# Token-major recurrence inputs, merge blocks between the recurrence's parts, modulation pieces moved, and a fixed order of the up products

## The chip, the cores and the metric

The kernel runs on one core of one Trainium2 chip. The metric is the device time of one execution in microseconds (us). The kernel before was timed three times: 1805.51 us is the median, 1804.99 to 1805.75 the range. A further execution was recorded by the profiler; all rows below come from it.

## The reference, cut to what matters

One block of a hybrid network on 256 tokens of width 2048, all in float32:

```python
mod = silu(c) @ ada_w + ada_b            # six vectors: sh1, sc1, g1, sh2, sc2, g2
h = rmsnorm(x, norm1_g) * (1 + sc1) + sh1
q, kc, vc, ks, vs, kw, vw, gates, lx, ly, ga, gb = split(h @ w_in)
o_a = nsa_attention(q, kc, vc, ks, vs, kw, vw, gates, ...)   # 16 heads, 4 groups
u = causal_dwconv(lx, conv_w, conv_b)
o_b = gelu(ly) * rg_lru(u, w_a, b_a, w_i, b_i, lam)          # a scan over the tokens
merged = sigmoid(ga) * (o_a @ proj_a) + sigmoid(gb) * (o_b @ proj_b)
x = x + g1 * (merged @ w_out)
h = rmsnorm(x, norm2_g) * (1 + sc2) + sh2
gate, val = split(h @ w_up)
x = x + g2 * ((gelu(causal_dwconv(gate)) * val) @ w_down)
return rmsnorm(x, final_g)
```

`lx` and `ly` are 2048 wide each. The recurrence wants them with the features on the partitions and the tokens along the row, since its scan runs along the row. `proj_a` needs the attention alone, `proj_b` the recurrence alone, the gates `ga` and `gb` only `h`.

## The kernel before

**How a weight is used.** Every weight comes from HBM in pieces of 128x2048 floats (1 MB) into a ring of four buffers `raw`. `stage` (line 95) issues the load on SP's queue; all loads keep their program order there. `split` (line 100) makes of each half piece (128x1024) a rounded part `hi` (ScalarE, line 107) and a rest `lo` (VectorE, line 108); three buffers of each exist. A product in the chip's float32r form is then three terms: `hi` of one side with `hi` and `lo` of the other, and `lo` with `hi`. The activations `h1`, `oA`, `oB`, `mg`, `h2` lie in SBUF with their rounded part in columns 0 to 255 (one per token) and the rest in columns 256 to 511.

**Two forms of a product.** Feature-major: the weight is the stationary side (128x128), the tokens move, and the result has features on the partitions. `dense_pair` (line 114) does so with one matmul of 512 columns (`hi` against both halves of the tokens, line 130) and one of 256 (`lo`, line 131). `dense_pair1` (line 171) makes 256 output features in one PSUM bank, by three matmuls of 256 columns for each weight tile (lines 184, 186, 187): 24 for each half piece. Token-major: `dense_tok` (line 191) has the tokens stationary and 512 columns of the weight moving; it makes 512 output features for 256 tokens in two banks by 12 matmuls of 512 columns for each half piece (lines 202 to 204), so 96 for the four pieces of one block. The dense products share four PSUM banks (tag "d", line 112), given out in turn; a bank comes free when the engine that empties it has read it.

**Stages.** Keys, values, queries and the first gate columns (`mq`) come first, then attention in eight units (`attention(g, t)`, four head groups by two token halves) beside the last quarter of those products and the products for `lx` (loop at line 682: eight pairs, each with two pieces, the bank copied by ScalarE in line 684). The recurrence follows in four parts `bt` of 512 features (line 694): a convolution on VectorE, two small float32 products for its gates (lines 713, 715), sigmoid, tanh, exp and sqrt on ScalarE (their order fixed by `tbl`, as each change of function loads a table), scans on VectorE, then twice a `dense_pair1` for `ly`, its gelu (line 735), the product with the scan, and the split into `oB`. Then the merge (line 749): for each of four output blocks `n` of 512 features and for each side `s`, the gate (for `n` = 0 already in `mq`, otherwise a `dense_tok`), its sigmoid (line 760), the projection by `dense_tok`, their product (line 763); the two sides are added and turned by float32 transposes on PE (line 774) into `mg`. `w_out`, the up products (`up`, line 151; 42 of the 48 by `dense_pair`) and the down products follow.

**Modulation pieces.** The first two of the six vectors are needed at once; the other 64 pieces (`filler`, `ada_piece`, line 230) take a `raw` buffer and 1 MB of load each and are multiplied and summed by VectorE alone (line 233). Before, 16 stand in the `lx` loop, 4 in the recurrence, 28 in the merge (in twos and fours behind a projection), 16 in the up stage.

**Order.** Each engine runs its instructions in one fixed order. A list scheduler with a timing model sets it when the kernel is built, from program order and priorities (`high_priority`); only what `keep_in_program_order` names keeps the order of the text.

## Time and profile before

| | us |
|---|---|
| median of 3 runs | 1805.51 (1804.99 to 1805.75) |
| the profiled execution's own time | 1807.09 |
| its span, first to last instruction | 1804.9 |
| PE busy | 1784.9 (99%) |
| weight loads busy | 1556.1 (86%) |
| VectorE (DVE) busy | 1340.6 (74%) |
| ScalarE (ACT) busy | 870.4 (48%) |
| HBM traffic | 429.51 MB moved, mean 238 GB/s |

PE is TensorE's matmuls, PEld its weight loads, which overlap them. Matmuls are pipelined: the duration of one is longer than the distance from its start to the next start, so a busy share of 99% doesn't say how many products were streamed in that time; the distance of starts does.

### The profile page before, as it was taken

Reading aid. Unit: us, or ns where it says so; the run is one execution under the profiler, and the core shown is the slowest. Engines: PE = TensorE matmul, PEld = TensorE weight load, DVE = VectorE, ACT = ScalarE, POOL = GpSimd, SP = SyncE. Lnnn points to the kernel's source line nnn. Section 1 sums busy time; section 2 is a strip of 40 time slices with the busy share of each in tenths; the row PEclk is TensorE's granted clock in tenths of the full one; section 3 lists DMA queues with packets and bytes.
Section 4 is the critical chain, followed back from the end, with each engine's and each line's share of the span. In section 5 each row is a group of like instructions: output and inputs, shape, how many; then the busy total and the mean of one; then the engine's idle time right before and its main releaser. Section 6 shows DMA issues by size and latency. Waiting matters only on the chain.

```text
span 1804.9 us, 25840 instructions
## 1 busy us (share of the span) xinstructions
PE 1784.9 (99%) x10336; PEld 1556.1 (86%) x10336; DVE 1340.6 (74%) x1955; ACT 870.4 (48%) x1185; POOL 0.2 (0%) x4
## 2 busy tenths in 40 slices
PE   8999999999999999999999999999999999999998
PEld 7899898888999888888888998888888888888886
DVE  7999876988788766766765997888545666666555
ACT  5644534655578443444445644444433444444443
POOL 0000000000000000000000000000000000000000
PEclk9999999999999999999999999999999999999999
DMA  9999863666546867787775566777655555555553
GB/s 352 362 329 366 312 239 118 210 222 219 215 170 227 289 241 288 289 287 280 292 276 198 184 227 238 274 280 279 244 187 196 189 190 191 188 189 188 186 191 113
DMA packets 64201, 429.51 MB, mean 238 GB/s; under 512 B 7089, under 2 KB 7377, under 8 KB 15569
## 3 DMA queue, kind: packets, MB, share of 16 engines
q1 hardware_dynamic: 63792, 427.08, 66.4%
q8 instruction: 81, 1.33, 0.3%
q10 hardware_dynamic: 288, 0.79, 0.1%
q14 instruction: 40, 0.32, 0.0%
HBM read 425.72 MB, written 2.11 MB: 237 GB/s over the span
## 4 chain that ended last, share of the span: by engine, by line
PE 92%; DVE 3%; DMA 2%; ACT 2%; issue 1%; DVEq 0%; ACTq 0%
PE P L130 17%; PE P L203 12%; PE P L204 11%; PE P L202 11%; PE P L131 9%; PE P L186 3%; PE P L187 3%; PE P L184 3%; PE P L437 2%; PE P L439 2%; PE P L438 2%; PE P L431 1%; PE P L432 1%; PE P L430 1%; DMA raw<-ada_w 1%; PE P L148 1%
## 5 line engine op out<-in xcount | busy, mean ns | idle before, releaser
L108 DVE TENSOR_TENSOR lo<-raw,hi 128x1024 fp32r<-128x1024 f32 x589 | 717.9, 1221 | 385.8 <-ACT hi L107 384.4
L107 ACT ACTIVATE hi<-raw 128x1024 fp32r<-128x1024 f32 x589 | 622.8, 1060 | 789.6 <-PE P L204 313.0
L130 PE MATMUL P<-h,hi 128*128 128x512 f32 x1344 | 465.9, 397 | 0.0
L131 PE MATMUL P<-h,lo 128*128 128x256 f32 x1344 | 362.8, 280 | 0.0
L130 PEld LDWEIGHTS P<-h,hi 128*128 128x128 f32 x1344 | 246.8, 188 | 53.2
L131 PEld LDWEIGHTS P<-h,lo 128*128 128x128 f32 x1344 | 253.6, 189 | 7.7
L233 DVE SCALAR_TENSOR_TENSOR raw<-raw,crow 128x2048 f32<-128x2048 f32 x64 | 146.3, 2286 | 7.2 <-DMA raw<-ada_w 6.4
L187 PE MATMUL P<-h,lo 128*128 128x256 f32 x512 | 147.6, 289 | 0.8 <-DVE lo L108 0.8
L186 PE MATMUL P<-h,hi 128*128 128x256 f32 x512 | 146.7, 287 | 0.0
L184 PE MATMUL P<-h,hi 128*128 128x256 f32 x512 | 146.7, 287 | 0.0
L437 PE MATMUL P<-h,hi 128*128 128x256 f32 x384 | 108.3, 286 | 0.0
L438 PE MATMUL P<-h,hi 128*128 128x256 f32 x384 | 107.5, 284 | 0.0
L439 PE MATMUL P<-h,lo 128*128 128x256 f32 x384 | 102.0, 283 | 0.0
L187 PEld LDWEIGHTS P<-h,lo 128*128 128x128 f32 x512 | 97.8, 191 | 1.8 <-DVE lo L108 1.4
L186 PEld LDWEIGHTS P<-h,hi 128*128 128x128 f32 x512 | 97.9, 191 | 1.4 <-issue 1.2
L184 PEld LDWEIGHTS P<-h,hi 128*128 128x128 f32 x512 | 97.9, 191 | 1.0 <-issue 0.7
L203 PE MATMUL P<-lo,ua 128*128 128x512 f32 x240 | 93.4, 389 | 0.0
L204 PE MATMUL P<-hi,ua 128*128 128x512 f32 x240 | 93.4, 389 | 0.0
L202 PE MATMUL P<-hi,ua 128*128 128x512 f32 x240 | 83.6, 389 | 0.0
L203 PE MATMUL P<-lo,h 128*128 128x512 f32 x192 | 75.5, 393 | 0.6 <-DVE lo L108 0.6
L204 PE MATMUL P<-hi,h 128*128 128x512 f32 x192 | 74.9, 390 | 0.0
L437 PEld LDWEIGHTS P<-h,hi 128*128 128x128 f32 x384 | 74.1, 193 | 0.2
(272 smaller groups left out, 3122.5 us busy)
## 6 DMA issues: line engine op xcount, KB each, us to landing
raw<-ada_w SPq DMA_DIRECT2D x96, 1024.0 KB, 5.1
raw<-w_up SPq DMA_DIRECT2D x96, 1024.0 KB, 4.9
raw<-w_down SPq DMA_DIRECT2D x48, 1024.0 KB, 4.9
raw<-w_lru SPq DMA_DIRECT2D x32, 1024.0 KB, 5.0
raw<-w_proj SPq DMA_DIRECT2D x32, 1024.0 KB, 5.0
raw<-w_gates SPq DMA_DIRECT2D x24, 1024.0 KB, 7.3
raw<-w_out SPq DMA_DIRECT2D x16, 1024.0 KB, 5.0
raw<-w_kv SPq DMA_DIRECT2D x24, 512.0 KB, 6.9
```

Source lines behind the costliest of these rows:

```text
L107: A.activation(hi[:, :n], raw[:, lo_col:lo_col + n], AF.Copy)
L108: V.tensor_tensor(lo[:, :n], raw[:, lo_col:lo_col + n], hi[:, :n].bitcast(F32), op=ALU.subtract)
L130: PE.matmul(ps[f], hi[:, sl], r, start=(kt == 0), stop=False, skip_group_check=True)
L131: PE.matmul(o, lo[:, sl], r[:, 0:256], start=False, stop=(kt == n - 1), skip_group_check=True)
L184: PE.matmul(o, hi[:, sl], r[:, 0:256], start=(kt == 0 and f == 0), stop=False, skip_group_check=True)
L186: PE.matmul(o, hi[:, sl], r[:, 256:512], start=False, stop=False, skip_group_check=True)
L187: PE.matmul(o, lo[:, sl], r[:, 0:256], start=False, stop=(kt == n - 1), skip_group_check=True)
L202: PE.matmul(ps[j], xh, hi[:, w], start=(kt == 0), stop=False, skip_group_check=True)
L203: PE.matmul(ps[j], xh, lo[:, w], start=False, stop=False, skip_group_check=True)
L204: PE.matmul(ps[j], xl, hi[:, w], start=False, stop=(kt == n - 1), skip_group_check=True)
L233: V.scalar_tensor_tensor(raw, raw, 1.0, row, op0=ALU.mult, op1=ALU.mult, accum_out=modc[:, c:c + 1])
L437: PE.matmul(o, hi[:, sl], h1[:, kt, 0:256], start=first and f % 2 == 0, stop=False, skip_group_check=True)
```

## The change

- `lx` and `ly` are made by `dense_tok`, in four blocks of 512 features each; the weights are laid out for it on the host. Each block's two banks are copied to SBUF by ScalarE (for `ly` by the gelu) and turned by the new `turned`, eight float32 transposes into two more banks of the same four. For `lx` ScalarE copies the turned banks out; for `ly` VectorE multiplies them with the scan straight from PSUM. `dense_pair1` is gone.
- Merge blocks stand between the parts of the recurrence: behind part 0 the projection of the attention for `n` = 0, behind part 1 the gate (1, 0), whose sigmoids run among those of part 2, behind part 2 the projection of the attention for `n` = 1. The sigmoids of `mq` run among those of part 0.
- Modulation pieces: 7 stand with the last key, value and gate products, 9 with `lx`, 32 in merge blocks, each behind a single piece of a `dense_tok` (two or three in a block); 16 remain for the up stage as before.
- In `dense_pair` the order of the matmuls is written out and kept: with two `hi` products at first in the first half piece, in plain alternation in all others.

The `w_lru` loads stay 32 pieces of 1 MB.

```diff
-        def dense_pair(pieces, rhs, narrow=False):
+        def dense_pair(pieces, rhs):
...
-                    hi, lo = split(raw, half * 1024, 1024)
...
+                    hl = split(raw, half * 1024, 1024)
+                    done = [0, 0]
+                    for w in (0, 0, 1, 0, 1, 0, 1, 1) + (0, 1) * 4 if ip + half == 0 else (0, 1) * 8:
+                        f, k = done[w] // 4, done[w] % 4
+                        done[w] += 1
+                        kt = ip * 8 + half * 4 + k
+                        r = rhs(kt)
+                        tc.keep_in_program_order(
+                            PE.matmul(ps[f][:, 0:256] if w else ps[f], hl[w][:, k * 256 + f * 128:k * 256 + f * 128 + 128],
+                                      r[:, 0:256] if w else r, start=(kt == 0 and not w), stop=(kt == n - 1 and w == 1),
+                                      skip_group_check=True))
...
-        def dense_pair1(pieces, rhs):
...
-        def dense_tok(pieces, lhs, late=None):
+        def dense_tok(pieces, lhs, late=None, fills=()):
...
+                if ip in fills:
+                    filler()
...
+        def turned(rows):
+            ps = [bank("turn"), bank("turn")]
+            for f in range(4):
+                for j in range(2):
+                    o = (f % 2) * 256 + j * 128
+                    PE.transpose(ps[f // 2][:, o:o + 128], rows[:, j, f * 128:f * 128 + 128], ident)
+            return [p.rearrange("p (f t) -> p f t", f=2) for p in ps]
...
         for i in range(4):
             whole(i, 3)
+            filler()
...
             whole(8 + b, 3)
+            filler()
...
-        for pr in range(8):
-            pl = dense_pair1([w_lru[pr, k] for k in range(2)], h1r)
-            A.activation(lx[pr // 2][:, 2 * (pr % 2):2 * (pr % 2) + 2],
-                         pl.rearrange("p (f t) -> p f t", f=2), AF.Copy)
-            if units:
-                attention(*units.pop(0))
-            filler(2)
...
+        for bt in range(4):
+            ps = dense_tok([w_lru[bt, k] for k in range(4)], h1r, fills=(1, 3))
+            rows = lx[bt].rearrange("p (j a) t -> p j (a t)", j=2)
+            for j in range(2):
+                A.activation(rows[:, j], ps[j], AF.Copy)
+            for h, p in enumerate(turned(rows)):
+                A.activation(lx[bt][:, 2 * h:2 * h + 2], p, AF.Copy)
+            for _ in range(2):
+                if units:
+                    attention(*units.pop(0))
+        assert not units
+        filler()
...
+        FILLS = (1, 3)
...
+        def open_gates(n, s, ps):
+            for j in range(2):
+                tbl(A.activation(gated[n, s][j], ps[j], AF.Sigmoid))
+
+        def multiply(n, s):
+            rhs = (lambda kt: oB[kt // 2][:, kt % 2]) if s else (lambda kt: oA[:, kt])
+            ps = dense_tok([w_proj[n, s, k] for k in range(4)], rhs, fills=(0, 1, 3) if s else FILLS)
+            for j in range(2):
+                V.tensor_tensor(gated[n, s][j], ps[j], gated[n, s][j], op=ALU.mult)
+
+        waiting = [(0, s, gates_of(0, s)) for s in range(2)]
...
+            while waiting:
+                open_gates(*waiting.pop(0))
             tbl(A.activation(r, r, AF.Exp, scale=-2.0))
...
-            for h in range(2):
+            ps = dense_tok([w_lru[4 + bt, k] for k in range(4)], h1r)
+            rows = u.rearrange("p (j a) t -> p j (a t)", j=2)
+            for j in range(2):
+                tbl(A.activation(rows[:, j], ps[j], AF.Gelu_apprx_tanh))
+            for h, p in enumerate(turned(rows)):
                 pr = bt * 2 + h
-                pl = dense_pair1([w_lru[8 + pr, k] for k in range(2)], h1r)
                 gl = u[:, 2 * h:2 * h + 2]
-                tbl(A.activation(gl, pl.rearrange("p (f t) -> p f t", f=2), AF.Gelu_apprx_tanh))
-                V.tensor_tensor(gl, gl, iu[:, 2 * h:2 * h + 2], op=ALU.mult)
+                V.tensor_tensor(gl, p, iu[:, 2 * h:2 * h + 2], op=ALU.mult)
...
-                filler(2 if pr % 4 == 0 else 0)
+            if bt == 1:
+                waiting.append((1, 0, gates_of(1, 0)))
+            elif bt < 3:
+                multiply(bt // 2, 0)
...
-                filler(2 if n == 0 else 4)
+            for s in range(2):
+                if (n, s) not in gated:
+                    open_gates(n, s, gates_of(n, s))
+                if s == 1 or n > 1:
+                    multiply(n, s)
```

## Rows read from the trace of the kernel before

**Rows 1.** The head of the page: the span, then busy time, share of the span and instruction count of each engine, and of the 40 equal slices the line with the granted TensorE clock (tenths of full speed).

```profile
span 1804.9 us, 25840 instructions
PE 1784.9 (99%) x10336; PEld 1556.1 (86%) x10336; DVE 1340.6 (74%) x1955; ACT 870.4 (48%) x1185; POOL 0.2 (0%) x4
...
PEclk9999999999999999999999999999999999999999
```

**Rows 2.** Busy time by stretch: the stretch and its length, then busy time and instruction count of PE, of the weight loads, of DVE, ACT and POOL, then the granted clock, the share of the 16 DMA engines and GB/s. The first stretch is attention beside the products for lx, the second the recurrence beside the products for ly, the others are single blocks of the merge (the last with eight transposes in it).

```profile
330.50:480.00 149.50, 149.00 (x1049) 126.77 (x1048) 130.49 (x353) 87.77 (x216) 0.00 (x0) 1.00 0.61 214
480.00:593.00 113.00, 112.18 (x872) 108.66 (x871) 95.98 (x136) 85.41 (x112) 0.00 (x0) 1.00 0.58 205
...
659.20:681.00 21.80, 21.80 (x98) 18.04 (x97) 17.09 (x18) 9.22 (x10) 0.00 (x0) 1.00 0.85 312
...
724.50:747.30 22.80, 22.80 (x105) 18.75 (x104) 14.65 (x20) 10.30 (x13) 0.00 (x0) 1.00 0.73 276
```

**Rows 3.** Groups of instructions by line: line, engine, operation, output<-inputs, shape, count | busy us, mean ns of one | idle before them and what ended it.

```profile
L108 DVE TENSOR_TENSOR lo<-raw,hi 128x1024 fp32r<-128x1024 f32 x589 | 717.9, 1221 | 385.8 <-ACT hi L107 384.4
L107 ACT ACTIVATE hi<-raw 128x1024 fp32r<-128x1024 f32 x589 | 622.8, 1060 | 789.6 <-PE P L204 313.0 <-PE P L130 242.3 <-PE P L438 42.6
...
L184 PE MATMUL P<-h,hi 128*128 128x256 f32 x512 | 146.7, 287 | 0.0
...
L233 DVE SCALAR_TENSOR_TENSOR raw<-raw,crow 128x2048 f32<-128x2048 f32 x64 | 146.3, 2286 | 7.2 <-DMA raw<-ada_w 6.4
...
L204 PE MATMUL P<-hi,h 128*128 128x512 f32 x192 | 74.9, 390 | 0.0
...
L774 PE MATMUL turn<-cols,sg 128*128 128x128 f32 x24 | 4.1, 272 | 0.0
```

**Rows 4.** Timeline of PE: start us, duration us, instruction. The first and the last start of an unbroken stretch of feature-major products; 120 matmuls (five halves of 24) start from the one up to the other.

```profile
489.00 0.28 PE L186 MATMUL P<-h,hi 128*128 128x256 f32 x1
...
503.40 0.28 PE L186 MATMUL P<-h,hi 128*128 128x256 f32 x1
```

**Rows 5.** The same for one token-major block: its first start and that of the block behind it, 96 matmuls later (4 pieces of two halves of 12).

```profile
659.22 0.62 PE L202 MATMUL P<-hi,oA 128*128 128x512 f32 x2
...
680.98 0.62 PE L202 MATMUL P<-hi,h 128*128 128x512 f32 x2
```

**Rows 6.** Timeline of PE around four transposes in a merge block.

```profile
740.04 0.39 PE L204 MATMUL P<-hi,h 128*128 128x512 f32 x1
740.27 0.60 PE L774 MATMUL turn<-cols,sg 128*128 128x128 f32 x4
740.63 0.48 PE L203 MATMUL P<-lo,h 128*128 128x512 f32 x1
740.95 0.40 PE L204 MATMUL P<-hi,h 128*128 128x512 f32 x1
```

**Rows 7.** Timeline of PE at the four places where it stood longest between 330 and 902 us; in brackets the idle time that the profile shows and what ended it.

```profile
336.26 0.28 PE L187 MATMUL P<-h,lo 128*128 128x256 f32 x1
337.03 0.66 PE L657 MATMUL tp<-cols,p 128*128 128x128 f32 x4 [0.50 <-ACT pcT L629]
...
559.67 0.28 PE L186 MATMUL P<-h,hi 128*128 128x256 f32 x1
560.60 0.39 PE L187 MATMUL P<-h,lo 128*128 128x256 f32 x1 [0.65 <-DVE lo L108]
...
769.10 0.61 PE L202 MATMUL P<-hi,h 128*128 128x512 f32 x2
769.87 0.50 PE L203 MATMUL P<-lo,h 128*128 128x512 f32 x1 [0.15 <-DVE lo L108]
...
857.59 0.63 PE L202 MATMUL P<-hi,h 128*128 128x512 f32 x2
858.64 0.50 PE L203 MATMUL P<-lo,h 128*128 128x512 f32 x1 [0.43 <-DVE lo L108]
```

**Rows 8.** The chain of waits that ended last, in order of time, from the stretches before those four places: start us, length us, what.

```profile
334.09 1.28 ACT L760
...
534.67 4.83 DMA raw<-ada_w
...
760.25 7.14 DMA raw<-w_gates
```

**Rows 9.** The activations around the recurrence: duration (lowest, median, highest ns), and the first and last start.

```profile
L719 ACT ACT_TABLE_LOAD  x4: 1283/1283/1283, 474.1 to 568.1; - x4
...
L735 ACT ACTIVATE lt<-P x8: 577/590/602, 504.3 to 594.1; 128x512 f32<-128x512 f32 x8
L735 ACT ACT_TABLE_LOAD  x4: 1283/1283/1283, 503.0 to 583.9; - x4
```

**Rows 10.** Timeline of PE in the up products: a stretch of 5 pairs that begins with two hi products and ends with two lo products, and the 12 alternating pairs behind it, up to the last start shown.

```profile
1401.94 0.62 PE L130 MATMUL P<-h,hi 128*128 128x512 f32 x2
1403.69 0.40 PE L130 MATMUL P<-h,hi 128*128 128x512 f32 x1
...
1407.93 0.40 PE L130 MATMUL P<-h,hi 128*128 128x512 f32 x1
```

**Rows 11.** Busy time by stretch (columns as in Rows 2), around the last key, value and gate products.

```profile
220.00:240.00 20.00, 20.00 (x125) 18.11 (x124) 17.40 (x43) 11.47 (x15) 0.00 (x0) 1.00 1.00 403
...
260.00:280.00 20.00, 20.00 (x129) 17.79 (x129) 9.20 (x12) 4.47 (x6) 0.00 (x0) 1.00 0.39 138
```

More of the change, by code (lines that the diff above doesn't have):

```diff
@@ L169, in up @@
             return take
-        def dense_pair1(pieces, rhs):
-            p = bank()
-            n = len(pieces) * 8
-            for ip, ap in enumerate(pieces):
-                raw = stage(ap)
-                for half in range(2):
-                    hi, lo = split(raw, half * 1024, 1024)
-                    for f in range(2):
-                        o = p[:, f * 256:f * 256 + 256]
-                        for k in range(4):
-                            kt = ip * 8 + half * 4 + k
-                            sl = slice(k * 256 + f * 128, k * 256 + f * 128 + 128)
-                            r = rhs(kt)
-                            PE.matmul(o, hi[:, sl], r[:, 0:256], start=(kt == 0 and f == 0), stop=False,
-                                      skip_group_check=True)
-                            PE.matmul(o, hi[:, sl], r[:, 256:512], start=False, stop=False, skip_group_check=True)
-                            PE.matmul(o, lo[:, sl], r[:, 0:256], start=False, stop=(kt == n - 1),
-                                      skip_group_check=True)
-            return p
-        def dense_tok(pieces, lhs, late=None):
+        def dense_tok(pieces, lhs, late=None, fills=()):
             ps = [bank(), bank()]
@@ L749, in block_kernel @@
         for n in range(4):
[L750 to L765 removed]
+            for s in range(2):
[3 more added lines that the diff above has]
+                    multiply(n, s)
+            m = [gated[n, s] for s in range(2)]
             if n == 2:
@@ L956, in _layout @@
     a["cmp_w2"] = np.stack([f["cmp_w2_k"][0], f["cmp_w2_v"][0]], axis=1)
-    a["w_lru"] = np.concatenate([_pack(w[:, 5168:7216]), _pack(w[:, 7216:9264])])
+    a["w_lru"] = _tok(w[:, 5168:9264])
     lw = np.stack([f["lru_wa"][0], f["lru_wi"][0]], axis=1).reshape(4, 4, 2, 128, 128)
```

39 lines of the change are left out of this document (10 added, 29 removed).

## The prediction

> **What bounds the kernel now.** I read the head of the page first: PE is busy for 1784.9 of 1804.9 us, at the full clock in every slice, while VectorE is busy for 74% and ScalarE for 48% [rows 1]. That alone doesn't say that PE is the bound, since durations of matmuls overlap, so the timeline comes next, for the distance of starts. In an unbroken stretch of feature-major products 120 matmuls of 256 columns take 503.40 - 489.00 = 14.40 us, 0.120 us each [rows 4]; a token-major block takes 680.98 - 659.22 = 21.76 us for 96 matmuls of 512 columns, 0.227 us each [rows 5]. These repeat without a gap: PE really streams. The third view is the timeline at the places where it doesn't. Between 330 and 902 us, the part that the change rewrites, the four worst are a distance of 0.77 us where 0.12 is usual (0.65 lost), 0.93 against 0.12 (0.81 lost), 0.77 against two of 0.227 (0.32 lost) and 1.05 against two of 0.227 (0.60 lost) [rows 7]. Together 2.4 us. So PE's own stream is the path, and the change is worth what it takes out of that stream, plus at most some 2.4 us of stalls. VectorE is full in the attention stretch (130.5 of 149.5 us) and less so in the recurrence (96.0 of 113.0) [rows 2], but there it runs beside PE, not ahead of it.
>
> **Part 1: lx and ly token-major.** It removes 16 feature-major pairs of blocks, each 2 pieces x 2 halves x 24 matmuls = 96 of 256 columns, so 192 for 512 features: 192 x 0.120 = 23.04 us. It puts eight token-major blocks there, 21.76 us each. Gain 1.28 us a block, 10.2 us in all. The number of pieces, of splits (hi 1.06 us on ScalarE, lo 1.22 us on VectorE, [rows 3]) and of loads stays. The same work costs less because a matmul of twice the columns takes 1.89 times as long: something like 13 ns a matmul is fixed in both forms.
>
> The Trainium skill, "TensorE: Matmul & The Clock Gate", section "Back-to-back issue gap", puts an isolated warm matmul at its columns over 2.4 GHz plus 2.5 ns: 215.8 ns for 512 columns, 109.2 for 256. By that the gain would be 768 x 2.6 ns = 2.0 us and not 10.2, and the whole sum would come out some 4 us slower than before. The rows differ (227 and 120 ns), and the measurement decides.
>
> **Part 2: the turning.** Eight transposes a block, 64 in all, are new on PE. Four of them in the merge begin at 740.27, the next product at 740.63, and that one takes 0.32 us to the start of its successor instead of 0.227: 0.36 + 0.09 = 0.45 us for four [rows 6]. Eight in one run cost between 0.36 x 2 + 0.09 = 0.81 and 0.90 us; a merge block with eight of them in it took 22.80 us against 21.80 without [rows 2], which is 1.0 in smaller groups. I take 0.90 a block, 7.2 us in all (6.5 to 8.0). Parts 1 and 2 together: -10.2 + 7.2 = -3.0 us. The copies that the turning adds on ScalarE (four of some 0.59 us [rows 9] for each lx block where there were two, no more gelus than before) lie beside products: ScalarE is busy for 87.8 of 149.5 us there [rows 2].
>
> **Part 3: stalls that go.** The first (0.65 us) is a transpose of attention that waits for ScalarE, which had just loaded a table for the sigmoids of mq [rows 7, 8]; these now stand among the sigmoids of part 0, so that load goes. The second (0.81) comes when VectorE has waited 4.83 us in its queue for a modulation piece, with splits behind it [rows 8]; the recurrence's own part has no pieces now. The third and fourth (0.32 and 0.60) stand behind pieces in fours, where four `raw` buffers are all taken and the next gate weight takes 7.14 us to land [rows 8]; pieces now come singly. I take all of it, -2.4 us; the other end is 0, if single pieces make VectorE wait as well. In a block with three pieces VectorE needs 8 x 1.22 + 3 x 2.29 = 16.6 us of 21.8 [rows 3, 5], so there is room.
>
> **Part 4: seven pieces with the last key, value and gate products.** There VectorE is busy for 9.2 of 20 us and the DMA for 0.39 at 260 to 280 us [rows 11]. Seven pieces need 7 x 2.29 = 16 us of VectorE over some 60 us and seven loads. Ahead of it, at 220 to 240 us, the queues are full (1.00, 403 GB/s [rows 11]), so loads drawn ahead now come later by one piece (1.05 MB at 403 GB/s is 2.6 us); the two halves that are already split, 5 us of products, hide that. I take 0; the other end is one piece late, +2.6. In return the attention stretch loses seven pieces (16 us of a VectorE that is full there), which speeds attention and, since PE has products to run meanwhile, pays nothing directly: below, 0 to -1.
>
> **Part 5: banks.** A lx or ly block takes two of the four banks, its turned copy the other two, so the block behind it begins in the banks that ScalarE is just emptying. Products for the first bank come first: six, 1.36 us. The second bank needs one copy, 0.59 us, and at worst a hi split in front of it, 1.06: 1.65 us, so 0.3 us late. ScalarE is busy for 9.2 of 21.8 us of a block [rows 2], so I take 0.42 x 8 x 0.3 = +1.0 us (0 to 2.4).
>
> **Part 6: merge blocks moved, up products in fixed order.** The merge blocks are the same 96 matmuls wherever they stand, and their loads (four of 1 MB a block) move with them on SP's queue, where the recurrence stretch moves only 205 GB/s [rows 2] against the 403 that the chip reaches [rows 11]: 0, and up to one late piece (2.6 us) if the queue order is worse. For ly VectorE reads the turned banks where it read SBUF; it isn't the bound there: 0. In the up stage 5 pairs that begin with two hi and end with two lo products took 1.75 us (0.350 a pair), 12 alternating ones 4.24 us (0.353) [rows 10]: 17 ns for a group. 42 of the 168 half pieces have that form afterwards. If all had it before, it costs 126 x 17 ns = 2.1 us; if none had, it gains 0.7. I take +0.5.
>
> **Sum.** -10.2 + 7.2 - 2.4 + 0 + 1.0 + 0.5 = -3.9 us. The profiled execution took 1807.09 us, 2.2 more than its span, and becomes 1803.2. The median of the runs is 1.6 us lower, 1805.51, and becomes 1801.6. The best ends of all terms give -10.2 + 6.5 - 2.4 - 1 - 0.7 = -7.8.
>
> **Rivals.** *Stalls only move.* Part 3 gives nothing and part 5 its full 2.4: -10.2 + 7.2 + 2.4 + 0.5 = -0.1, 1805.4 us. For it: VectorE is as loaded as before. Against: three of the four stalls have a cause in the text that is gone.
>
> *More comes out.* The best ends: about 1798.5. For it: attention and the recurrence both get slack.
>
> *The first part's chain holds the banks (slower).* The ly banks are free only after the gelu, which must follow sigmoid, tanh, exp and sqrt of its part; the turned banks are the other two, so PE can't run ahead. From the table load for the first sigmoid to the first gelu it took 504.3 - 474.1 = 30.2 us in part 0, and 585.2 - 568.1 = 17.1 in the last part [rows 9]. Later parts have a merge block and the ly block in front of their gelu, 43.5 us, so they never wait. Part 0 has only its ly block, 22.7 us with the turning, and four sigmoids of mq more (2.4 us): 9.9 us late if its sigmoids start with the block, so 1811.5 us. It decides from 3.9 us on, that is when they start less than 6 us ahead of the ly block. Against: attention, which keeps the same banks and tiles, should end earlier.
>
> *Transposes wait (slower).* If the eight stand right behind their block, PE waits for a split and a copy, 1.65 us, eight times: 13.2 instead of 1.0, 1813.8 us. It is slower than before from 0.6 us a block. For it: the first stall above was such a transpose. Against: in the merge they were put among products without a gap [rows 6].
>
> *A transpose costs its duration.* 272 ns [rows 3] x 64 = 17.4 us instead of 7.2: 1811.8 us. Against: four started within 0.36 us [rows 6]. The Trainium skill, same page, section "Part 4: PE-mode transpose", says about 275 ns in one kernel, and that the full clock doesn't engage in this mode; by it 17.6 us. The clock in the merge stretch with eight of them was 1.00, the 2.4 GHz level [rows 2], so I give it little.
>
> **How the numbers follow.** 0.2% is 3.6 us, about what a measurement of this kernel can tell from no change: faster is below 1801.9, slower above 1809.1. Forecast 0.47 (its own range 1799.5 to 1804, some 0.6 of it below 1801.9), more comes out 0.17, stalls move 0.20, the chain of part 0 0.07, waiting transposes 0.06, full duration 0.03. Faster 0.28 + 0.17 = 0.45, slower 0.16, the same 0.39. The range runs from 1797.5 to 1810.
>
> **What would show it.** Token-major lx and ly blocks of 21.8 us; runs of eight transposes within 0.9 us and a next product of 0.31; no distance over 0.3 us at the table loads of attention or behind pieces. Part 5 shows as a wait of PE for ScalarE's copy or gelu at a block's first product in the second bank. The forecast is wrong if PE stands for microseconds in front of the first ly block's transposes, if the transposes stand apart in pairs, or if the up pairs come to more than 0.355 us.

## The result and the profile after

The changed kernel takes 1826.91 us (median of 4 runs, 1826.24 to 1828.85); the kernel before, beside it on the same chip, 1805.63. The ratio is 1.0117, 95% interval 1.0104 to 1.0131: slower by 21 us, where 1801.6 was forecast. In the profiled executions the span went from 1804.9 to 1824.4 us. The head of the page after, to be held against [rows 1]:

```profile
span 1824.4 us, 24418 instructions
PE 1787.2 (98%) x9632; PEld 1521.0 (83%) x9632; DVE 1342.9 (74%) x1955; ACT 873.1 (48%) x1191; POOL 0.2 (0%) x4
...
PEclk9999999999989999999999999999999999999999
```

There are 704 matmuls fewer (1536 of 256 columns gone, 768 of 512 columns and 64 transposes new), and PE is as busy as before in a span that is 20 us longer. The digit 8 in the clock's line is new.

Where the time came in: the products of `w_out` begin at 925.6 us instead of 901.8, so +23.8 up to there; the up products give 4.9 back; the rest of the run differs by 0.6. The first view after is busy time by stretch, columns as in [rows 2]:

```profile
330.50:480.00 149.50, 147.25 (x700) 108.91 (x699) 115.62 (x310) 82.01 (x200) 0.00 (x0) 1.00 0.48 171
...
463.00:485.40 22.40, 18.15 (x75) 10.28 (x74) 18.07 (x64) 15.28 (x42) 0.00 (x0) 0.93 0.12 46
485.40:490.00 4.60, 4.60 (x15) 3.70 (x14) 0.00 (x0) 0.00 (x0) 0.00 (x0) 0.58 0.00 0
...
515.80:524.40 8.60, 0.37 (x3) 0.02 (x1) 2.68 (x3) 8.54 (x11) 0.00 (x0) 0.74 0.69 283
524.40:530.00 5.60, 5.60 (x15) 4.45 (x16) 5.23 (x7) 1.36 (x2) 0.00 (x0) 0.50 0.06 11
```

VectorE does less in the attention stretch than before (115.6 us against 130.5 in [rows 2]), so the pieces did leave it, and attention still didn't get faster. The matmul of `oT` with `cmpb`, once in each of the eight units, marks its pace. This is the view of that tile, with the first and the last start behind the durations; before:

```profile
L661 PE MATMUL oT<-pcT,cmpb x8: 491/501/502, 313.2 to 468.9; 47*128 47x512 f32 x8
```

and after:

```profile
L658 PE MATMUL oT<-pcT,cmpb x8: 491/497/502, 311.0 to 481.6; 47*128 47x512 f32 x8
```

Seven units took 155.7 us and now take 170.6. The second to the fifth of these intervals were 20.8 to 21.9 us and are 26.8 to 30.5. In each stood 93 to 111 dense matmuls of 256 columns; now there stand 78 to 85, of 512 columns. At 463 us the last product of `lx` is done, and attention still has some 43 us to go. Its last step into `oA` starts at 483.3 us before (the second time in each line is the start of the last one):

```profile
L670 DVE TENSOR_TENSOR oA<-oT,oA x8: 679/686/693, 336.5 to 483.3; 128x512 fp32r<-128x512 f32 x8
```

and at 506.8 us after:

```profile
L667 DVE TENSOR_TENSOR oA<-oT,oA x8: 670/692/694, 331.5 to 506.8; 128x512 fp32r<-128x512 f32 x8
```

From 463 until 485.4 us PE stands in gaps of 0.2 to 1.3 us, 4.2 us in all, and the DMA falls to 46 GB/s.

The second loss is in the timeline of PE, in front of the first `ly` block's transposes:

```profile
515.54 0.39 PE L185 MATMUL P<-lo,h 128*128 128x512 f32 x1
515.77 0.39 PE L186 MATMUL P<-hi,h 128*128 128x512 f32 x1
524.38 0.69 PE L215 MATMUL turn<-cols,lt 128*128 128x128 f32 x2 [8.23 <-ACT lt L759]
524.72 0.78 PE L184 MATMUL P<-hi,oA 128*128 128x512 f32 x1
525.30 0.63 PE L185 MATMUL P<-lo,oA 128*128 128x512 f32 x1
525.73 0.63 PE L186 MATMUL P<-hi,oA 128*128 128x512 f32 x1
526.15 0.63 PE L184 MATMUL P<-hi,oA 128*128 128x512 f32 x1
...
576.69 0.39 PE L186 MATMUL P<-hi,h 128*128 128x512 f32 x1
576.92 0.40 PE L184 MATMUL P<-hi,h 128*128 128x512 f32 x1
...
579.21 0.82 PE L215 MATMUL turn<-cols,lt 128*128 128x128 f32 x6
579.78 0.48 PE L184 MATMUL P<-hi,h 128*128 128x512 f32 x1
...
635.17 0.61 PE L184 MATMUL P<-hi,oA 128*128 128x512 f32 x2
636.91 0.50 PE L185 MATMUL P<-lo,oA 128*128 128x512 f32 x1 [1.13 <-DVE lo L108]
```

PE stood 8.23 us for the gelu (line 759). The products behind it start 0.427 us apart where 0.227 is usual, twelve of them with the first (0.58), in a stretch with a granted clock of 0.50, the 1.2 GHz level; eight more do so from 485.5 to 489.1. That adds some 20 x 0.2 = 4 us. The Trainium skill, "TensorE: Matmul & The Clock Gate", section "Back-to-back issue gap", gives the columns over 1.2 GHz as the distance at the lower level. An estimate by it for 512 columns is 426.7 ns; the trace agrees with 0.427 us. The chain of waits shows what the gelu waited for:

```profile
512.97 0.47 ACT lt L743
...
515.12 0.52 ACT lt L746
...
516.04 1.67 ACT mq L706 x3
517.71 0.01 issue
517.72 1.28 ACT L749
...
520.07 1.28 ACT L750
...
522.44 1.28 ACT L759
523.72 0.01 issue
523.73 0.61 ACT lt L759
524.34 0.04 issue
524.38 0.69 PE turn L215 x2
```

In order: sigmoids of the recurrence (743), tanh (746), four sigmoids of `mq` (706), and table loads of 1.28 us for exp (749), sqrt (750) and gelu (759), all behind attention that ended late. The third loss stands in the groups of VectorE, the line that answers to L233 in [rows 3]:

```profile
L227 DVE SCALAR_TENSOR_TENSOR raw<-raw,crow 128x2048 f32<-128x2048 f32 x64 | 146.5, 2289 | 45.5 <-DMA raw<-ada_w 45.5
```

VectorE waits 45.5 us for pieces where it waited 6.4, in 32 waits of at most 3.3 us. The splits behind such a wait are late, as at 636.91 in the timeline; seven waits of PE like this one, 0.6 to 1.7 us each, make 7 us.

The sum: distances of starts over 0.45 us between 330 and 902 us are 28 with 31.4 us in all, before 9 with 5.6. Less 0.2 us each that a product takes anyway, PE stood 22 us longer. With 4 us at the lower clock and less the 3.0 us that products and turning give, that makes +23 of the +23.8 us.

### The profile page after: what moved, and what is told of

Same layout as the page of the kernel before. It is cut to its first block, busy times and chain, and to the rows that moved or that the text cites. A ratio compares the mean times of both kernels' runs of the same rounds, so it can differ in the third digit from the quotient of the medians.

```text
span 1824.4 us, 24418 instructions
## 1 busy us (share of the span) xinstructions
PE 1787.2 (98%) x9632; PEld 1521.0 (83%) x9632; DVE 1342.9 (74%) x1955; ACT 873.1 (48%) x1191; POOL 0.2 (0%) x4
## 4 chain that ended last, share of the span: by engine, by line
PE 83%; DMA 7%; DVE 4%; issue 2%; ACT 2%; DVEq 0%; ACTq 0%
PE P L130 26%; PE P L185 11%; PE P L186 11%; PE P L184 11%; DMA raw<-ada_w 7%; PE P L431 2%; PE P L432 2%; PE P L433 2%; DVE raw L227 2%; PE P L425 2%; PE P L426 1%; PE P L424 1%; DVE lo L108 1%; PE P L149 1%; PE P L148 1%
## 5 line engine op out<-in xcount | busy, mean ns | idle before, releaser
L130 PE MATMUL P<-h,lo 128*128 128x256 f32 x1344 | 366.4, 278 | 0.0
L130 PEld LDWEIGHTS P<-h,hi 128*128 128x128 f32 x1344 | 249.1, 188 | 54.9
L130 PEld LDWEIGHTS P<-h,lo 128*128 128x128 f32 x1344 | 252.4, 188 | 4.2
L185 PE MATMUL P<-lo,h 128*128 128x512 f32 x448 | 179.0, 400 | 2.0 <-DVE lo L108 1.9
L227 DVE SCALAR_TENSOR_TENSOR raw<-raw,crow 128x2048 f32<-128x2048 f32 x64 | 146.5, 2289 | 45.5 <-DMA raw<-ada_w 45.5
L186 PE MATMUL P<-hi,h 128*128 128x512 f32 x448 | 176.3, 393 | 0.0
L184 PE MATMUL P<-hi,h 128*128 128x512 f32 x448 | 165.4, 397 | 0.0
L431 PE MATMUL P<-h,hi 128*128 128x256 f32 x384 | 108.2, 286 | 0.0
L432 PE MATMUL P<-h,hi 128*128 128x256 f32 x384 | 107.4, 284 | 0.0
L185 PEld LDWEIGHTS P<-lo,h 128*128 128x128 f32 x448 | 84.6, 189 | 21.9 <-DVE lo L108 4.8
L433 PE MATMUL P<-h,lo 128*128 128x256 f32 x384 | 101.9, 284 | 0.0
L186 PEld LDWEIGHTS P<-hi,h 128*128 128x128 f32 x448 | 84.6, 189 | 17.5 <-issue 0.7
L184 PEld LDWEIGHTS P<-hi,h 128*128 128x128 f32 x448 | 84.6, 189 | 17.0
L431 PEld LDWEIGHTS P<-h,hi 128*128 128x128 f32 x384 | 74.2, 193 | 0.2
L432 PEld LDWEIGHTS P<-h,hi 128*128 128x128 f32 x384 | 74.2, 193 | 0.0
L316 DVE SCALAR_TENSOR_TENSOR raw<-raw,crow 128x2048 f32<-128x2048 f32 x31 | 70.8, 2286 | 2.0 <-DMA raw<-ada_w 1.8
```

The costliest lines, as they stand in the source:

```text
L130: PE.matmul(ps[f][:, 0:256] if w else ps[f], hl[w][:, k * 256 + f * 128:k * 256 + f * 128 + 128], r[:, 0:256] if w else r, start=(kt == 0 ...
L184: PE.matmul(ps[j], xh, hi[:, w], start=(kt == 0), stop=False, skip_group_check=True)
L185: PE.matmul(ps[j], xh, lo[:, w], start=False, stop=False, skip_group_check=True)
L186: PE.matmul(ps[j], xl, hi[:, w], start=False, stop=(kt == n - 1), skip_group_check=True)
L227: V.scalar_tensor_tensor(raw, raw, 1.0, row, op0=ALU.mult, op1=ALU.mult, accum_out=modc[:, c:c + 1])
L316: V.scalar_tensor_tensor(raw, raw, 1.0, crow, op0=ALU.mult, op1=ALU.mult, accum_out=mc)
```

## The experiments

All times are medians beside runs of the kernel before on the same chip (1805.8 to 1807.4 us). The runs were made on several chips, so that two of them are compared by their ratios to the kernel before; the changed kernel's is 1.0117 (1.0104 to 1.0131), and a difference of less than some 0.002 between two ratios is not told from none.

**e1: the up order alone.** The kernel before with the new `dense_pair`, nothing else.

> The kernel before with one part of the change alone: the written order of the up products. In the profile of the changed kernel 1344 pairs of the up stages took 467.1 us, before 472.0. Theory U (the order itself is worth it, my term of +0.5 us was wrong in sign): 1800.7 us, 4.9 less than before. Rival (the pairs got faster through something else that changed, such as where the buffers lie or which splits run beside them): within 1 us of before, and pairs of 0.351 us.

1801.32 us, ratio 0.9970 (0.9958 to 0.9982). This one edit gains 5 us; everything else together costs 26.

**e2: the turned `ly` in PSUM banks of its own**, in the changed kernel.

```diff
...
-            ps = [bank("turn"), bank("turn")]
+            ps = [psx.tile([128, 512], F32, tag="s", bufs=2, name="turn") if own else bank("turn") for _ in range(2)]
...
```

> The changed kernel with the turned ly in the recurrence's own two banks (tag s) and no longer in the four banks of the dense products. Theory B (the ring of four banks is the cause: two with ly until the gelu, two with its turned copy, so PE stands 8.4 us in front of the first turning and then runs 12 matmuls at the lower clock, 2.4 us): these 10.8 us and three waits of 0.5 us go, 1814.5 us against 1826.9, and the projection of attention runs ahead of the turning. Rival P (PE has nothing ready there anyway, since the projection waits for attention or for VectorE): the wait only changes its place, 1825 to 1828.

1819.99 us, 1.0068 (1.0047 to 1.0088). Some 7 us come back, between the two expectations. The wait at the first turning shrinks from 8.2 to 2.8 us: with two banks free, PE runs on into the next block. The waits at 463 to 485 us remain.

**e3: pieces in twos and fours, as before.**

```diff
...
-            ps = dense_tok([w_proj[n, s, k] for k in range(4)], rhs, fills=(0, 1, 3) if s else FILLS)
+            ps = dense_tok([w_proj[n, s, k] for k in range(4)], rhs)
...
+            filler(2 if n == 0 else 4)
...
```

> The changed kernel with the modulation pieces where they stood before (none with the key, value and gate products; 16 with lx, 4 with ly, twos and fours behind a whole projection). Theory F (a single piece behind one weight piece is loaded only when VectorE has freed a buffer, VectorE then waits for it with the next split behind it; VectorE waits 45.5 us for such loads where it waited 6.4 before, and PE stands 7 us for splits between 600 and 860 us): 1820 us, with VectorE's wait for pieces under 15 us. Rival (the clumps make PE wait as much as the single ones): within 2 us of 1826.9; or slower, if the 9 pieces more in attention's stretch cost what VectorE lacks there.

1825.42 us, 1.0104 (1.0084 to 1.0124). VectorE waits 9.7 us for pieces instead of 45.5, as it should, and PE's waits behind 690 us go; others in the recurrence take their place (2.5 us at 611 us, 0.9 at 558, 621 and 667), and the first turning waits 9.4 us. The single pieces make the waits that they are seen at, but taking them away alone is worth 1.5 us by the medians, which the two intervals don't tell from nothing: the rival's time.

**e4: `lx` feature-major again**, in the changed kernel.

```diff
...
-            ps = dense_tok([w_lru[bt, k] for k in range(4)], h1r, fills=(1, 3))
...
+            pl = dense_pair1([w_lru[pr // 2, 2 * (pr % 2) + k] for k in range(2)], h1r)
...
```

> The changed kernel with lx feature-major as before, in one bank each, eight pairs with one piece and one attention unit behind each of the first four; ly stays token-major. Theory L (the lx blocks run ahead of attention, which ends at 506 us instead of 483, and the last of them holds two banks from 463 to 484 us because its memory is that of attention's compressed values; PE stands 5 us there and runs 18 matmuls at the lower clock): attention ends near 483 us, that stretch has no stall, and 8 us come back less the 1.5 us that token-major lx is worth: 1820. If the lateness of attention also makes the 8.4 us wait at the first ly block, that shrinks too: down to 1812. Rival (attention is late for another reason, such as its place in the order): 1827 or above.

1820.10 us, 1.0070 (1.0055 to 1.0085), as expected. Seven units of attention take 149.6 us (313.0 to 462.6), less than before the change, and no wait stands at 463 to 485 us. Other waits come up behind it, 3.5 us at 496 us the longest.

**e5: `lx` token-major, but by two matmuls of 256 columns for each of 512.**

```diff
...
+                    if narrow:
+                        for c in range(2):
+                            o, w = ps[j][:, c * 256:c * 256 + 256], slice(k * 512 + c * 256, k * 512 + c * 256 + 256)
+                            PE.matmul(o, xh, hi[:, w], start=(kt == 0 and c == 0), stop=False, skip_group_check=True)
...
```

> The changed kernel with the matmuls of the lx blocks cut to 256 columns: 192 of them a block instead of 96, everything else (two banks, turning, memory, program order) as changed. In the trace before, 88 to 111 dense matmuls stand between two units of attention in PE's order, 21 to 22 us a unit; in the changed one 78 to 85, but of 512 columns, 27 to 30 us a unit, so that lx is used up after five units and the last two stand uncovered. Theory M (the order gives about as many matmuls to a unit whatever their width, so wide ones stretch attention): units of 21 to 23 us, attention ends near 485 us instead of 506, no stall over 0.3 us at 463 to 485 us, and though PE gets 5 us more of products, the time falls to some 1817. Theory L (banks and the memory that lx shares with attention make the stall): the stall stays, units stay at 27 us or more, and the time rises by 5 us to 1832.

1822.73 us, 1.0097 (1.0082 to 1.0112). The seven units take 148.8 us (312.4 to 461.2): the same blocks, transposes and banks, and attention is back at its pace. PE has 5 us more of products, and yet the time is 4 us lower (the two intervals overlap a little). A wait of 3.5 us for a split at 502.7 us and those for single pieces stay, so the time was missed by 6 us.

**e6: e2, and the memory of `lx`'s last block free from the start.** The fourth `lx` tile shares memory with `cmpb`, which attention reads to its end; here `cmpb` lies elsewhere, and the tiles `pT` make room for it.

```diff
...
-        cmpb = big.tile([128, 1024], F32R, tag="C7", name="cmpb")
+            cmpb = big.tile([128, 1024], F32R, tag="C2", name="cmpb")
...
```

> The run with the turned ly in its own banks (1820.0), and attention's compressed values moved to memory that the last lx block doesn't use, so that this block's two banks come free at 463 us and not at 484. Theory L: ly products fill the stretch from 463 to 485 us, where PE stands 5 us and then runs 18 matmuls at the lower clock; 8 us come back, 1812. Theory M: the stall at 463 to 485 us can shrink, but the end of attention (506 us) and the part 0 behind it stay as late as they are, so PE stands later instead, at the first ly block's turning or the products behind it: 1817 to 1821.

1815.20 us, 1.0057 (1.0042 to 1.0072), 4.8 less than e2 by the medians. The two intervals overlap; in the profiled executions `w_out` begins 4.2 us earlier (913.7 against 917.9). The stretch 463 to 490 us in e2:

```profile
463.00:490.00 27.00, 22.74 (x89) 13.95 (x88) 18.18 (x64) 15.30 (x42) 0.00 (x0) 0.87 0.09 36
```

and in e6:

```profile
463.00:490.00 27.00, 27.00 (x126) 19.60 (x124) 15.67 (x45) 13.90 (x33) 0.00 (x0) 1.00 0.33 118
```

So a memory wait was part of it: in the changed kernel ScalarE copied the last `lx` block only at 483.7 us, 20 us after its products were done, and two of the four banks were held meanwhile. In e6 that copy starts at 463.2 us. Attention got no faster by it but slower: products of `ly`, 512 columns wide, now stand beside the last two of the seven units measured (28.0 and 30.4 us, in e2 21.1 and 10.9), and it ends 21.5 us later than in e2 (506.9 us there):

```profile
L670 DVE TENSOR_TENSOR oA<-oT,oA x8: 669/690/692, 332.9 to 528.4; 128x512 fp32r<-128x512 f32 x8
```

The kernel is no slower for it, since `ly` now covers that end. So it is less the late end of attention that costs time than attention with nothing beside it.

**e7: merge blocks behind the recurrence, as before.**

```diff
...
-            elif bt < 3:
-                multiply(bt // 2, 0)
...
```

> The changed kernel without merge blocks between the parts of the recurrence: all of them behind it, in the order of before; the sigmoids of mq stay in part 0. If the alternation hides the chain of the recurrence behind a merge block, as it says, PE now waits at each ly block's turning: a part took 17 us from its first sigmoid to its gelu, a ly block is 22.7 us, so parts 1 to 3 still fit and it costs nothing, or 2 to 4 us where VectorE is late; 1825 to 1831. Rival: the alternation itself costs, through its single pieces and the gate (1, 0) that part 2 must wait for: 1820 to 1823.

1823.66 us, 1.0107 (1.0090 to 1.0124), 3 us less than with the alternation by the medians, 2 by the ratios, which the two intervals don't tell from nothing. The first turning waits 4.8 us instead of 8.2. The blocks between the parts hide nothing that was open.

**e8: the edits with no product in them on the kernel before**: e1, the sigmoids of `mq` among those of part 0, and the recurrence's four pieces moved ahead.

> The kernel before with the written order of the up products (1801.3), the sigmoids of mq among those of part 0, and the four modulation pieces of the recurrence moved to the last key and value products; lx and ly stay feature-major, the merge stays behind. Three of the four long stalls of the trace before were put down to these places (0.65 at the table load, 0.81 at the pieces in the recurrence, each with about 0.1 us behind it): 1799.7. If stalls only move: 1801 to 1802.

1801.65 us, 0.9981 (0.9972 to 0.9990): the same as e1, so the stalls only moved. Waits went and came elsewhere (0.9 us at 524, 1.1 at 552, 0.7 at 901).

**e9 and e10: one token-major edit each on e1.** `ly` in e9 (turned in banks of its own), `lx` in e10, pieces as before.

> The kernel before with the written order of the up products (1801.3) and ly alone token-major, its turned copy in the recurrence's own two banks; lx, the place of the merge and of the pieces as before. Theory M: attention isn't touched (units of 21 us, end at 483 us), so the change of form is worth what its products say: four blocks at 1.28 us less, eight transposes of 0.9 us more: -1.5, 1799.8. Theory B: a ly block takes two of the four banks until its gelu, so PE runs ahead by one block where it ran ahead by four half blocks; part 0 took 30 us to its gelu and a ly block 22.7, so PE stands up to 7 us once: 1801 to 1807.

> The kernel before with the written order of the up products (1801.3) and lx alone token-major and turned, as in the changed kernel; ly feature-major in one bank each, pieces in clumps, merge behind. Theory M: units of attention go from 21 to 27 us and more, attention ends past 500 us, the tail of it stands uncovered or the recurrence behind it is late: 1808 to 1815, that is the larger part of the change's loss from this edit alone. Rival (lx token-major is harmless where ly has four one-bank blocks to run ahead): 1799 to 1802.

e9: 1809.30 us, 1.0018 (1.0008 to 1.0027), 8 over e1. e10: 1821.42 us, 1.0097 (1.0079 to 1.0114), 20 over e1. By products and turning (-5.1 + 3.6) each should have been 1.5 below; both lie above the ranges expected. The distances over 0.45 us between 330 and 902 us add up to 4.7 us in e1, 14.8 in e9 and 23.1 in e10, so in e9 the excess is nearly all waiting. In e10 most of it is, and some 3 us come from products at the lower clock (granted 0.50 from 538.0 to 544.8 us, where products of 256 columns start 0.21 us apart, not 0.12); its longest wait, 4.9 us at 534.5 us, is for a split behind the recurrence's first part. In e9 PE waits in the recurrence for splits and for the gelu ahead of the turning; the groups of 490 to 615 us:

```profile
L204 PE MATMUL P<-lo,h 128*128 128x512 f32 x124 | 49.5, 399 | 2.7 <-DVE lo L108 2.7
...
L232 PE MATMUL turn<-cols,lt 128*128 128x128 f32 x32 | 4.9, 275 | 2.7 <-ACT lt L745 2.7
```

**e11 and e12: the parts undone together**, both with banks of their own for the turned `ly` and pieces in twos and fours: e11 with `lx` feature-major, e12 with e6's memory.

> The changed kernel with lx feature-major, the turned ly in its own banks and the pieces in clumps: of the change there remain ly token-major, the alternation with merge blocks and the up order. It differs from the run with ly alone by the alternation and the sigmoids of mq. If the alternation is worth something once nothing else stands in its way: 1797 to 1800. If it costs because the gate (1, 0) holds up part 2 and the pieces behind a merge block make VectorE late: 1802 to 1808.

> The run with lx token-major, the compressed values moved and the turned ly in its own banks (1815.2), with the pieces in clumps. Theory F: 3 to 5 us of waits for splits behind single pieces go, 1811. By theory M attention stays late and this run stays above 1808. Rival (the waits for splits move into the recurrence, as in the run with clumps alone): 1814 to 1816.

e11: 1814.55 us, 1.0052 (1.0037 to 1.0067). e12: 1816.92 us, 1.0065 (1.0050 to 1.0080), nothing gained over e6. Both missed. e11 is e9 with the alternation of merge blocks and the sigmoids of `mq` added, measured on the same chip: 1814.55 against 1809.30 us, ratios 1.0052 and 1.0018. So the alternation costs some 5 us here (e8 has the same sigmoids, on the kernel before, for nothing); which wait makes these 5 us wasn't taken apart. Once pieces, memory and banks are mended, waits for splits of 1 to 3 us stand in the recurrence in their place. No repair of the changed kernel came near 1805.

**e13 and e14: e10 and e9 with matmuls of 256 columns**, by the edit of e5.

> The kernel before with the written up order (1801.3 us alone) and lx alone token-major and turned (1821.4 us with matmuls of 512 columns), here by two matmuls of 256 columns for each of 512. The products of lx take what they took feature-major, 192 x 0.120 = 23.04 us a block, so over the first only the turning, 4 x 0.9 = 3.6 us, is added. Theory (the order gives a unit of attention about as many matmuls, whatever their width): units of attention back at 19 to 24 us, no stalls of microseconds at 463 to 490 us, 1805 to 1809 us. Rival (the two banks of a block and the two of its turning make PE wait, not the width): attention may tighten, but the stalls stay, 1816 us or more.

> The same for ly alone, which with 512 columns took 1809.3 us. Its products take 4 x 23.04 us instead of 4 x 21.76 us (+5.1). If the width of the matmuls makes the stalls of the recurrence too, they go (some 9 us), and the time is 1801.3 + 3.6 = 1805 us. Rival (the stalls come from the splits that stand behind the long operations of the recurrence on VectorE and from the gelu in front of the turning, whatever the width): 1809.3 + 5.1 = 1814 us.

e13: 1805.68 us, ratio 1.0000 (0.9990 to 1.0009); nothing differs from e10 but the width, and 15.7 us are gone. The marks of attention in e10:

```profile
L672 PE MATMUL oT<-pcT,cmpb x8: 491/498/792, 312.3 to 489.8; 47*128 47x512 f32 x8
```

and in e13:

```profile
L679 PE MATMUL oT<-pcT,cmpb x8: 492/500/502, 312.9 to 469.2; 47*128 47x512 f32 x8
```

177.5 us against 156.3 for seven units, and with the latter no wait of microseconds at 463 to 490 us. What e13 has over e1, 4.4 us by the medians and 5.8 up to `w_out` in the traces, is somewhat more than the price of turning (3.6). For `lx` the width is the cause. e14: 1810.80 us, 1.0027 (1.0016 to 1.0038), between the two expectations. Its products are 5.1 us longer than e9's and its median 1.5, but in the profiled executions `w_out` begins 5.8 us later (912.7 against 906.9). So it isn't shown that the width made any of `ly`'s waits: the wait at a turning (2.6 us at 572 us) and those for splits stayed, and the distances over 0.45 us went from 14.8 to 12.5 us in all. What of `ly`'s 8 us is VectorE's order and what the bank that the gelu holds wasn't taken apart further.

**e15 to e18: the up order.** e15 alternates plainly throughout; e16 begins each half piece with two hi products and ends it with two lo; e17 has the change's doubled group in the first two pairs of blocks alone, e18 at the start of each of the two runs of up products (down products stand between them). The line of e1, and what stands in its place in each run:

```diff
-                    for w in (0, 0, 1, 0, 1, 0, 1, 1) + (0, 1) * 4 if ip + half == 0 else (0, 1) * 8:
+                    for w in (0, 1) * 8:                    # e15
+                    for w in (0,) + (0, 1) * 7 + (1,):      # e16
+                    for w in (0, 0, 1, 0, 1, 0, 1, 1) + (0, 1) * 4 if ip + half == 0 and len(begun) < 2 else (0, 1) * 8:          # e17
+                    for w in (0, 0, 1, 0, 1, 0, 1, 1) + (0, 1) * 4 if ip + half == 0 and len(begun) in (0, 18) else (0, 1) * 8:   # e18
```

> The kernel before with up products in plain alternation in every half piece, the first included. The trace of the kernel before has half pieces of the same plain alternation at two speeds: 2.773 us (matmuls start 231, 112, 233, 117 ns after each other) and 2.831 us (233, 117, 241, 120, 236, 113 ns), and two hi products in a row change the one to the other. Theory: the alternation runs in one of two rhythms, and a doubled product or two decides which. Without any doubled product all half pieces take 2.773 us, the 42 that begin with two hi lose another 27 ns each (2.800 to 2.773), 1.1 us, and the time is 1800.2 us. Rival: the first half piece has no rest to run yet when it begins, and PE waits for it at some of the 42, 1801.3 us or more.

> The kernel before with another written up order: each half piece begins with two hi products and ends with two lo products, and alternates in between. Theory of the two rhythms: the doubled hi product puts the alternation in the slow one, the doubled lo product at the end takes it out again, so every half piece takes 2.81 to 2.83 us instead of 2.773 to 2.800: 168 x 0.04 = 7 us over the order of the change, about 1808 us. The prediction's reading (a pair in a group that begins with two hi costs 0.350 us, an alternating one 0.353): this order is the cheapest, 168 x 17 ns = 2.9 us less than plain alternation, so about 1799 us.

> The kernel before with the written up order, but with the group that begins with two hi and ends with two lo products in the first half piece of the first two pairs of blocks alone; all other half pieces in plain alternation. Theory: the group puts the alternation into the fast rhythm and nothing after it takes it out, so every half piece of the up products takes 2.773 us: 40 x 27 ns = 1.1 us less than with the group in each first half piece, up products 465.9 us where they took 467.0, and 1800.2 us. Rival (the rhythm falls back to the slow one at each new pair of blocks unless a group stands there): 2.826 us a half piece from the third pair on, as in plain alternation throughout, and 1809 us.

> As the run before, but with the group in the first half piece of the first pair of each of the two runs of up products (behind the first 18 pairs come down products, and there the alternation began in the slow rhythm). Theory: the rhythm is kept until other products stand between, so all half pieces but two take 2.773 us, 1.1 us less than with a group in each pair, and the time is 1800.2 us. Rival (what starts the second run in the slow rhythm isn't undone by one group): 1805.5 us as before.

e15: 1809.18 us, 1.0015 (1.0006 to 1.0024); e16: 1808.90, 1.0013 (1.0003 to 1.0022); e17: 1805.57, 0.9998 (0.9989 to 1.0007); e18: 1800.59, 0.9967 (0.9955 to 0.9979), the lowest ratio of all, though its interval doesn't tell it from e1. The kernel before shows both rhythms in one timeline of PE; from the first to the second of these lines, and from the third to the fourth, lie eight plain pairs each:

```profile
1088.21 0.39 PE L130 MATMUL P<-h,hi 128*128 128x512 f32 x1
...
1090.98 0.62 PE L130 MATMUL P<-h,hi 128*128 128x512 f32 x2
...
1093.80 0.40 PE L130 MATMUL P<-h,hi 128*128 128x512 f32 x1
...
1096.63 0.62 PE L130 MATMUL P<-h,hi 128*128 128x512 f32 x2
```

2.77 us and 2.83 us for the same work, at a granted clock of 1.00. The second stands behind a group with doubled products (the x2 at 1090.98). In e17 the first run of up products is in the fast rhythm and the second, behind other products, in the slow one; ten pairs in the first, then eleven in the second run:

```profile
1196.86 0.40 PE L132 MATMUL P<-h,hi 128*128 128x512 f32 x1
...
1200.33 0.40 PE L132 MATMUL P<-h,hi 128*128 128x512 f32 x1
...
1407.92 0.40 PE L132 MATMUL P<-h,hi 128*128 128x512 f32 x1
...
1411.80 0.40 PE L132 MATMUL P<-h,hi 128*128 128x512 f32 x1
```

0.347 us a pair and 0.353. e18, with one group more there, is fast throughout (2.774 us a half piece on average, 2.780 in e1: 1.1 us for 168 of them, as expected, and less than the times can tell). e16's expectation held: with two `hi` at each start and two `lo` at each end a half piece takes 2.820 us. e15's expectation was wrong in one point: without any doubled product the alternation doesn't fall into the fast rhythm, it stays in the one in which it begins, here the slow one (2.827 us a half piece on average). So the rhythm is a state that lasts until something breaks the alternation, and the change's order happens to set the fast one. By the half pieces that can be followed, before to e1: 2.808 to 2.780 us, times 168 is 4.7 us, nearly the whole gain. What in PE makes the two rhythms no run here shows.

## Why the prediction was wrong

**PE's stream is the path** held, and so did the prices of **parts 1 and 2**. The block from 553.37 us on starts its 96th product at 575.23, 0.230 us apart on average where 0.227 was taken; six transposes take 579.78 - 579.21 = 0.57 us, at a granted clock of 1.00 in stretches without a standstill. The rival that a transpose costs its duration is out: e13 has 32 of them for 4.4 us. What failed is the view that PE's stream stays gapless when these products change. One sum is off as well: the best ends of all terms, -7.8 from 1805.51, give 1797.7 us and not about 1798.5.

**Part 4** is the step with the largest error. "The attention stretch loses seven pieces ... which speeds attention" is wrong: attention ended 23 us later. The products of `lx` are the cover under which attention runs. The fixed order puts some four fifths as many of them beside a unit as before (78 to 85 against 93 to 111), each 1.9 times as long, while the blocks hold only half as many: the units stretch, the cover runs out at 463 us, and what is left of attention stands open. No term of the sum held this. That the width does it is shown by e5 and e13, and by e10 against e1 it is 20 us with its followers. That the order goes more by count than by time is read from the counts alone (the second to fifth units have 73 to 96 wide products beside them in the changed kernel and e10, 82 to 145 narrow ones in the kernel before, e4, e5 and e13); why the planner does so wasn't looked into.

**Part 5** took 0.3 us a block and +1.0 in all. The copies did fit, but the gelu is no copy: it waits for a chain of other functions. This is the rival "the first part's chain holds the banks", given 0.07, priced at 9.9 us, and measured at 8.23 plus 2.4 for the clock behind it; PE standing for microseconds there was one of the prediction's own signs of being wrong. Its "against", that attention ends earlier, was the same error as in part 4. The later parts were to wait "never"; they waited 0.5 us each, three times. A second holder of banks, the memory shared with `cmpb`, was not in the prediction at all; e6 puts it at some 4 us, within the noise of the two times but plain in the stretch shown (27.00 of 27 us busy, not 22.74).

**Part 3** took all four stalls as gone, -2.4. The first two are gone. Single pieces brought seven new waits, 7 us: "there is room" counted VectorE's busy time (16.6 of 21.8 us), not its order. The load of a piece is issued when a `raw` buffer comes free and takes 4.8 to 6.2 us to land at five places of the chain between 617 and 685 us; VectorE, which runs in order, stands up to 3.3 us for it with splits behind. A reading was wrong too: the 4.83 us of [rows 8] are such a load from issue to landing, not a wait of VectorE, which was busy beside it and stood 0.22 us, as its timeline before shows:

```profile
539.52 2.29 DVE L233 SCALAR_TENSOR_TENSOR raw<-raw,crow 128x2048 f32<-128x2048 f32 x1 [0.22 <-DMA raw<-ada_w]
```

So little of the second stall can come from that wait. e8 shows that removed stalls come back elsewhere even without the products, and e3 that undoing the pieces alone gains nothing clear of the noise.

**Part 6**: the merge blocks, taken at 0, cost some 5 us (e11 against e9), of which undoing them in the changed kernel gave back no more than 2 to 3 (e7). The up order, taken at +0.5, gave -4.9. The rows [rows 10] were read as a price of the doubled group against plain alternation; the twelve alternating pairs there, 0.353 us each, were plain alternation in its slow rhythm, and the fast one, 0.347, stood in the same trace 314 us earlier.

## What to carry to other kernels

A product that covers a stage which mostly waits for its own results is priced by what it covers: before making it cheaper or wider, count how many of its instructions stand beside a unit of that stage. The Trainium skill, "Perfetto Trace Analysis", section "Matmuls", says that larger matmuls are more efficient where possible; here a block of them is (21.8 us against 23.0), and the kernel with the smaller ones is 15.7 us faster (e13 against e10). A result that must be turned kept its banks here until the gelu, last in a chain of functions, had read them, and a price of an instruction order needs more than one place of the trace, since the same order ran at two speeds in one execution.

## What was not expected of the hardware

Plain alternation of 512- and 256-column products ran in two lasting rhythms, 2.773 and 2.82 to 2.83 us for eight pairs, at the same granted clock of 1.00. And two standstills cost more than their length: behind the 8.23 us the granted clock was 0.50, the 1.2 GHz level, and twelve products took 0.2 us more each; behind 22 us of short gaps (PE busy for 18.15 of 22.4) eight did.
